# The low parts of a down projection's weights: a VectorE subtraction, or a negated copy and an adding transfer

## The chip, the cores and the metric

The kernel runs on one core of a Trainium2 chip. The time is the device time of one execution, in microseconds (us). The kernel before has a median of 911.25 us over 3 runs (911.24 to 911.4). All durations of single instructions come from one profiled execution, which took 911.68 us.

The engines are named as in the profile: PE is TensorE's matmul and PEld its weight load, DVE is VectorE, ACT is ScalarE, POOL is GpSimd, and SP is SyncE, which only issues transfers here. A trailing q (SPq, POOLq) means the engine's sequencer.

## The reference

A decoder block for 512 tokens of width 1024: attention with a sliding window, beside a gated linear recurrence; both are merged, projected and added to the input; a SwiGLU feed-forward with 2816 hidden columns follows, then a last normalisation. What matters here is its end:

```
z = (jax.nn.silu(jnp.einsum('bsd,df->bsf', u, w_ffn_gate[layer]))
     * jnp.einsum('bsd,df->bsf', u, w_ffn_up[layer]))
h = h + jnp.einsum('bsf,fd->bsd', z, w_ffn_down[layer])
...
return rmsnorm(h, norm_final_g)
```

All inputs are float32, `w_ffn_down` has 2816 x 1024 elements (11 MiB).

## The kernel before

Every product is made in three matmuls of a shorter format (fp32r). Each operand x is split into a high part h, which is x rounded to fp32r, and a low part l = x - h; then h·h + h·l + l·h stands for the product.

The weights go through the class `Weights`. They are read from DRAM in units of 1 MiB (`load`, lines 55 to 68) by SP's queue into a tile `raw` with two buffers. A unit has two granules of 128x1024. `split` (lines 79 to 104) makes the high and the low tile of one granule: ScalarE copies `raw` to `wh` with rounding (line 98), and VectorE subtracts, `wl` = `raw` - `wh` (line 102). `wh` and `wl` have three buffers each. `get` (lines 106 to 112) hands out the granules in order and splits up to `AHEAD` = 2 granules ahead of the one handed out. `split` also asks for the unit of its own granule and for the next one (lines 81 to 83).

The units are listed at lines 149 to 166. The last eleven are of kind "f": two blocks of 128 rows of `w_ffn_down`, each row whole, 1024 columns. Their 22 granules are the row blocks f = 0 to 21 of the down projection. The units before them are of kind "c" (gate and up weights).

The feed-forward loop (lines 834 to 851) handles two blocks of hidden columns at a time: two gate granules (VectorE line 839, a sigmoid on ScalarE, two multiplications on GpSimd at lines 843 and 844), then two up granules (VectorE line 849, ScalarE line 850, VectorE line 851). The first two granules of the down projection are split beside its last two up granules.

The down projection has two parts. For f = 0 to 17 (lines 874 to 877) each granule feeds 24 matmuls: four blocks of 128 tokens, three terms, two halves of 512 columns (`down`, line 866; the matmul is line 870). [...] The last `TAIL_F` = 4 granules are split into four buffers of their own, from the pool `wd` (lines 878 to 880); with them the four token blocks are finished one after the other (lines 881 to 913): the residual (line 891), sums of squares on ScalarE (line 892), the multiplication with the last gain on GpSimd (line 904), the power on GpSimd (line 908), the scaling on three engines and the store.

The order of an engine's instructions follows a scheduler that keeps the data's dependencies and works by its own estimate of times; the order of the program sets the priorities.

Of the kernel before, what the change touches and what calls it, by code (L numbers as in the profile page):

```python
# [15 lines left out]
F32 = mybir.dt.float32  # L16
F32R = mybir.dt.float32r
U32 = mybir.dt.uint32
AF = mybir.ActivationFunctionType
ALU = mybir.AluOpType  # L20
AX = mybir.AxisListType

P = 128
# [17 lines left out]
class Weights:  # L41


    def __init__(self, nc, pool, units):
# [7 lines left out]
        self.done = 0  # L52
        self.pos = 0

    def load(self, u):
        if u >= len(self.units) or u in self.raw:
            return
        kind, w, c0 = self.units[u]
        t = self.pool.tile([P, 2048], F32, tag="raw", bufs=2, name=f"raw{u}")
        if kind == "f":  # L60
            self.nc.sync.dma_start(
                t.rearrange("p (f n) -> p f n", f=2),
                w[c0 * P:(c0 + 2) * P, :].rearrange("(f p) n -> p f n", p=P))
        else:
            self.nc.sync.dma_start(
                t.rearrange("p (k n) -> p k n", k=KD),
                w[:, c0:c0 + 256].rearrange("(k p) n -> p k n", p=P))
        self.raw[u] = t
# [10 lines left out]
    def split(self, i, pool=None, bufs=3, high=None, low=None, low_after=None):  # L79
        u, kind, half = self.grans[i]  # L80
        self.load(u)
        if u:
            self.load(u + 1)
        nc, raw = self.nc, self.raw[u]
        if kind == "c":
            src = raw.rearrange("p (k n) -> p k n", k=KD)[:, :, half * P:(half + 1) * P]
            shape = dict(k=KD)
        else:
            n = 256 if kind == "k" else 1024
            src = raw[:, half * 1024:(half + 1) * 1024].rearrange("p (k n) -> p k n", n=n)  # L90
            shape = dict(n=n)
        pool = pool or self.pool
        h = pool.tile([P, 1024], F32R, tag="wh", bufs=bufs, name=f"wh{i}")
        l = pool.tile([P, 1024], F32R, tag="wl", bufs=bufs, name=f"wl{i}")
        hv = h.rearrange("p (k n) -> p k n", **shape)
        lv = l.rearrange("p (k n) -> p k n", **shape)
        if high is None:
            nc.scalar.activation(hv, src, AF.Copy)  # L98
        else:
            high.tensor_copy(hv, src)  # L100
        with low_after or nullcontext():
            (low or nc.vector).tensor_tensor(lv, src, hv.bitcast(F32), ALU.subtract)  # L102
        self.ready[i] = (hv, lv)
        self.done = i + 1

    def get(self, limit=None):
        i = self.pos
        self.pos += 1
        last = min(i + AHEAD, len(self.grans) - 1 if limit is None else limit)
        while self.done <= last:  # L110
            self.split(self.done)
        return self.ready.pop(i)
# [836 lines left out]
```

## Time and profile before

| what | value |
|---|---|
| median of 3 runs | 911.25 us |
| the profiled execution | 911.68 us |
| its span, first to last instruction | 910.0 us |
| mean granted TensorE clock | 0.999 |
| read from HBM, written to HBM | 82.90 MB, 2.10 MB |
| TensorE in the stage of the down projection | first matmul at 783.3 us, last at 902.6 us |
| transfers issued by GpSimd | none |

The profile is read like this. A row of the timeline has the start, the duration, the engine, the line of the kernel, the operation, the tile written and the tiles read (`wl<-raw,wh`), the shapes, and in brackets how long the engine was idle before and which event ended that. A row of the groups has the number of instructions, then their busy time in us and the mean of one in ns, then the idle time before them by what ended it. A row of the transfers has their count, the size of one, and the median time from issue to landing. A row of the windows has each engine's busy time in that stretch, the granted clock, the mean busy share of the sixteen transfer engines, and GB/s. The chain goes back from the last instruction, at each step to what released it. Matmul rows overlap (each shows 389 ns, one starts every 227 ns), so the stage's time is read from starts.

### The profile page before, as it was taken

The numbers are of one execution on the slowest core, as the hardware profiler recorded it, in microseconds if no ns is written. First come the engines' busy times: TensorE is split into PE (matmuls) and PEld (weight loads), VectorE is DVE, ScalarE is ACT, GpSimd is POOL, SyncE is SP. The second block draws the span as 40 slices with busy tenths as digits, with TensorE's granted clock in tenths as the row PEclk, the third lists the DMA queues.
The fourth block names the chain that finished last, engine by engine and source line by source line (L and its number), as shares of the span: only waits on it lengthen the run. The fifth ranks groups of instructions, "written<-read, shape, count | busy, mean of one in ns | idle before, by whom it ended". The sixth has DMA issues, their size and how long they took to land.

```text
span 910.0 us, 11601 instructions
## 1 busy us (share of the span) xinstructions
PE 899.6 (99%) x4668; PEld 769.8 (85%) x4668; DVE 463.3 (51%) x725; ACT 371.0 (41%) x634; POOL 142.8 (16%) x148
## 2 busy tenths in 40 slices
PE   8999999999999999999999999999999999999996
PEld 7888889888898988888888998888888888888885
DVE  5677877647484755745345445334443334322314
ACT  6566775655453636215233443223322223211214
POOL 3003533300000000000000003222233322100004
PEclk9999999999999999999999999999999999999999
DMA  7321211322221141322243222232222333322212
GB/s 257 93 93 47 94 47 47 93 93 93 93 91 49 47 139 47 95 91 94 93 167 110 94 93 93 93 93 93 92 93 94 101 109 111 119 93 93 92 47 94
DMA packets 73522, 85.74 MB, mean 94 GB/s; under 512 B 1690, under 2 KB 68348, under 8 KB 73468
## 3 DMA queue, kind: packets, MB, share of 16 engines
q1 hardware_dynamic: 72876, 83.95, 28.6%
q10 hardware_dynamic: 592, 1.05, 0.3%
q8 instruction: 37, 0.61, 0.3%
q14 instruction: 17, 0.14, 0.0%
HBM read 82.90 MB, written 2.10 MB: 93 GB/s over the span
## 4 chain that ended last, share of the span: by engine, by line
PE 97%; SPq 1%; DMA 0%; POOL 0%; DVE 0%; issue 0%; ACT 0%; POOLq 0%; DVEq 0%
PE acc L870 13%; PE ps_big L362 13%; PE ps_big L363 13%; PE ps_big L364 13%; PE ps_f L364 9%; PE ps_f L363 9%; PE ps_f L362 9%; PE ps_o L374 2%; PE ps_v L373 2%; PE ps_o L373 2%; PE ps_o L372 2%; PE ps_v L374 2%; PE ps_v L372 2%; PE pv L498 1%; PE sc L442 1%; PE pa L619 1%
## 5 line engine op out<-in xcount | busy, mean ns | idle before, releaser
L98 ACT ACTIVATE wh<-raw 128x1024 fp32r<-128x1024 f32 x147 | 155.1, 1059 | 394.8 <-PE ps_f L363 161.8
L102 DVE TENSOR_TENSOR wl<-raw,wh 128x1024 fp32r<-128x1024 f32 x147 | 180.4, 1229 | 160.1 <-ACT wh L98 159.9
L362 PE MATMUL ps_big<-uh,wh 128*128 128x512 f32 x376 | 148.8, 396 | 0.0
L363 PE MATMUL ps_big<-ul,wh 128*128 128x512 f32 x376 | 147.8, 393 | 0.0
L364 PE MATMUL ps_big<-uh,wl 128*128 128x512 f32 x376 | 147.7, 393 | 0.0
L363 PE MATMUL ps_f<-u2l,wh 128*128 128x512 f32 x352 | 137.2, 390 | 0.0
L364 PE MATMUL ps_f<-u2h,wl 128*128 128x512 f32 x352 | 136.9, 389 | 0.0
L362 PE MATMUL ps_f<-u2h,wh 128*128 128x512 f32 x352 | 136.8, 390 | 0.0
L364 PEld LDWEIGHTS ps_big<-uh,wl 128*128 128x128 f32 x376 | 70.7, 188 | 14.2
L363 PEld LDWEIGHTS ps_big<-ul,wh 128*128 128x128 f32 x376 | 70.8, 188 | 13.6
L362 PEld LDWEIGHTS ps_big<-uh,wh 128*128 128x128 f32 x376 | 70.7, 188 | 13.5
L363 PEld LDWEIGHTS ps_f<-u2l,wh 128*128 128x128 f32 x352 | 66.1, 188 | 14.0 <-issue 0.2
L364 PEld LDWEIGHTS ps_f<-u2h,wl 128*128 128x128 f32 x352 | 66.1, 188 | 13.8 <-issue 0.2
L362 PEld LDWEIGHTS ps_f<-u2h,wh 128*128 128x128 f32 x352 | 66.1, 188 | 13.7
L843 POOL TENSOR_TENSOR zg<-zg,sgf 128x512 f32<-128x512 f32 x22 | 39.4, 1794 | 161.0 <-ACT sgf L134 161.0
L870 PE MATMUL acc<-wh,zl 128*128 128x512 f32 x176 | 56.9, 389 | 0.0
L870 PE MATMUL acc<-wl,zh 128*128 128x512 f32 x176 | 56.9, 389 | 0.0
L870 PE MATMUL acc<-wh,zh 128*128 128x512 f32 x176 | 56.8, 389 | 0.0
L849 DVE TENSOR_TENSOR zz<-ps_f,zg 128x512 f32<-128x512 f32 x22 | 15.2, 692 | 62.6 <-PE ps_f L364 61.5
L839 DVE TENSOR_TENSOR zg<-ps_f,R 128x512 f32<-128x512 f32 x22 | 15.1, 691 | 62.2 <-PE ps_f L364 62.2
L248 POOL TENSOR_TENSOR r<-ss,neghalf 128x4 f32<-128x4 f32 x8 | 10.1, 1260 | 232.8 <-DVE ss L247 232.8
L870 PEld LDWEIGHTS acc<-wh,zh 128*128 128x128 f32 x176 | 33.0, 188 | 6.9
(222 smaller groups left out, 1560.0 us busy)
## 6 DMA issues: line engine op xcount, KB each, us to landing
raw<-in_w_in_dram SPq DMA_DIRECT2D x27, 1024.0 KB, 5.2
raw<-in_w_ffn_gate_dram SPq DMA_DIRECT2D x11, 1024.0 KB, 5.0
raw<-in_w_ffn_up_dram SPq DMA_DIRECT2D x11, 1024.0 KB, 5.1
raw<-in_w_ffn_down_dram SPq DMA_DIRECT2D x11, 1024.0 KB, 4.8
raw<-in_w_branch_attn_dram SPq DMA_DIRECT2D x4, 1024.0 KB, 6.0
raw<-in_w_branch_hgrn_dram SPq DMA_DIRECT2D x4, 1024.0 KB, 4.9
raw<-in_w_out_dram SPq DMA_DIRECT2D x4, 1024.0 KB, 5.2
xt<-in_x_dram SPq DMA_DIRECT2D x4, 512.0 KB, 7.7
```

Source lines behind the costliest of these rows:

```text
L98: nc.scalar.activation(hv, src, AF.Copy)
L102: (low or nc.vector).tensor_tensor(lv, src, hv.bitcast(F32), ALU.subtract)
L362: pe.matmul(ps, wh[:, k, :], ah[:, k, :], start=k == 0, stop=False)
L363: pe.matmul(ps, wh[:, k, :], al[:, k, :], start=False, stop=False)
L364: pe.matmul(ps, wl[:, k, :], ah[:, k, :], start=False, stop=k == KD - 1)
L372: pe.matmul(ps, ah[:, k0 + k, ts], wh[:, k, :], start=first and k == 0, stop=False)
L373: pe.matmul(ps, ah[:, k0 + k, ts], wl[:, k, :], start=False, stop=False)
L374: pe.matmul(ps, al[:, k0 + k, ts], wh[:, k, :], start=False, stop=last and k == 3)
L839: tt(zg, fproject((lambda: row_broadcast(R, rstd2, u2pool)) if first else None), R, ALU.mult)
L843: pool_e.tensor_tensor(zg, zg, sg, ALU.mult)
L849: tt(z, fproject(), gs[a], ALU.mult)
L870: pe.matmul(acc[t][half], ah[:, f, ts], wv[:, 0, half * S:half * S + S], start=f == 0 and ah is zh and wv is wh, stop=f == NF - 1 and ah i ...
```

## The change

For the granules of kind "f", the 22 of the down projection, the low tile is made in another way. ScalarE writes -h to it (a copy of `wh` with scale -1), and a transfer issued by GpSimd adds the same weights, read once more from DRAM, onto the tile: l = -h + w. The high copy at line 98 and the load into `raw` stay. All other weights are split as before. Each of the 22 transfers moves 512 KB (128 rows of 4 KB).

```
--- before.py
+++ after.py
@@ -51,6 +51,8 @@
         self.ready = {}
         self.done = 0
         self.pos = 0
+
+        self.by_dma = next(u for u, k in enumerate(units) if k[0] == "f")
 
     def load(self, u):
         if u >= len(self.units) or u in self.raw:
@@ -98,10 +100,26 @@
             nc.scalar.activation(hv, src, AF.Copy)
         else:
             high.tensor_copy(hv, src)
-        with low_after or nullcontext():
-            (low or nc.vector).tensor_tensor(lv, src, hv.bitcast(F32), ALU.subtract)
+        if u >= self.by_dma:
+            self.hv = hv
+            self.low_by_dma(i, lv, src)
+        else:
+            with low_after or nullcontext():
+                (low or nc.vector).tensor_tensor(lv, src, hv.bitcast(F32), ALU.subtract)
         self.ready[i] = (hv, lv)
         self.done = i + 1
+
+    def low_by_dma(self, i, lv, src):
+
+        u, kind, half = self.grans[i]
+        _, w, c0 = self.units[u]
+        nc, hv = self.nc, self.hv
+        nc.scalar.activation(lv, hv.bitcast(F32), AF.Copy, scale=-1.0)
+        if kind == "c":
+            d = w[:, c0 + half * P:c0 + half * P + P].rearrange("(k p) n -> p k n", p=P)
+        else:
+            d = w[(c0 + half) * P:(c0 + half + 1) * P, :].rearrange("(f p) n -> p f n", p=P)
+        nc.gpsimd.dma_start(lv, d, accum_op=ALU.add)
 
     def get(self, limit=None):
         i = self.pos
```

## The prediction

> **What bounds the kernel now.** I read the page's head and its chain first, to see which engine sets the end.
>
> ```profile
> span 910.0 us, 11601 instructions
> ...
> PE 899.6 (99%) x4668; PEld 769.8 (85%) x4668; DVE 463.3 (51%) x725; ACT 371.0 (41%) x634; POOL 142.8 (16%) x148
> ...
> PE 97%; SPq 1%; DMA 0%; POOL 0%; DVE 0%; issue 0%; ACT 0%; POOLq 0%; DVEq 0%
> ```
>
> TensorE is busy for 99% of the span, and 97% of the chain that ended last is TensorE itself. So shorter work on another engine is worth something only where TensorE waits for it. The change touches the last stage alone; the view of windows and the chain in order of time show that stage.
>
> ```profile
> core 0: us, PE busy (x) PEld busy (x) DVE busy (x) ACT busy (x) POOL busy (x), PEclk, DMA share, GB/s
> 783.30:881.30 98.00, 98.00 (x435) 81.12 (x433) 25.70 (x24) 21.41 (x21) 0.00 (x0) 1.00 0.29 96
> 881.30:903.00 21.70, 21.69 (x96) 17.64 (x94) 8.79 (x25) 8.38 (x31) 8.59 (x10) 1.00 0.19 74
> ```
>
> ```profile
> 783.32 119.69 PE acc L870 x528
> 903.03 0.44 DVE yo L891
> ...
> 905.70 0.39 DVEq L945
> ```
>
> The reader is to see that TensorE has no gap between 783.30 and 903.00 (98.00 of 98.00 us, then 21.69 of 21.70), at granted clock 1.00. The down projection is one piece of the chain: 528 matmuls in 119.69 us, or 0.2267 us each. One row block f of its weights (a granule: one high and one low tile of 128x1024) feeds 24 of them, so a granule lasts 5.44 us. There is no wait that the change could remove, and its VectorE work is not in the chain. The 7 us behind the last matmul hold no granule's work.
>
> **What the change removes.** The groups of the window 789 to 876 us, where only this stage runs:
>
> ```profile
> L102 DVE TENSOR_TENSOR wl<-raw,wh 128x1024 fp32r<-128x1024 f32 x19 | 23.1, 1225 | 64.2 <-ACT wh L98 64.2
> L98 ACT ACTIVATE wh<-raw 128x1024 fp32r<-128x1024 f32 x19 | 19.9, 1059 | 67.4 <-PE acc L870 62.5 <-DMA raw<-in_w_ffn_down_dram 4.9
> ```
>
> Removed are 22 subtractions of 1.225 us, 27 us of VectorE. VectorE is busy for 25.70 of 98.00 us there and TensorE never waits for it, so they bring 0. Added are 22 ScalarE activations of the same shape as the high copies, at 1.059 us each: 23.3 us on an engine busy for 21.41 of 98.00 us. Both ops of a granule take 2.1 us of its 5.44, so ScalarE does not become the bound.
>
> **Steady state: the slack of a granule.** The timeline of ScalarE:
>
> ```profile
> 772.29 1.06 ACT L98 ACTIVATE wh<-raw 128x1024 fp32r<-128x1024 f32 x1 [3.85 <-PE ps_f L363]
> 773.26 0.63 ACT L134 ACTIVATE sgf<-zg 128x512 f32<-128x512 f32 x1
> 777.75 1.06 ACT L98 ACTIVATE wh<-raw 128x1024 fp32r<-128x1024 f32 x1 [3.85 <-PE ps_f L363]
> 778.71 0.63 ACT L129 ACTIVATE zh<-zz 128x512 fp32r<-128x512 f32 x1
> 783.17 1.06 ACT L98 ACTIVATE wh<-raw 128x1024 fp32r<-128x1024 f32 x1 [3.83 <-PE ps_f L363]
> ...
> 848.63 1.06 ACT L98 ACTIVATE wh<-raw 128x1024 fp32r<-128x1024 f32 x1 [4.38 <-PE acc L870]
> 854.07 1.06 ACT L98 ACTIVATE wh<-raw 128x1024 fp32r<-128x1024 f32 x1 [4.38 <-PE acc L870]
> 859.51 1.06 ACT L98 ACTIVATE wh<-raw 128x1024 fp32r<-128x1024 f32 x1 [4.38 <-PE acc L870]
> 861.41 2.01 ACT L98 ACTIVATE wh<-raw 128x1024 fp32r<-128x1024 f32 x2 [0.84 <-DMA raw<-in_w_ffn_down_dram]
> 864.95 1.06 ACT L98 ACTIVATE wh<-raw 128x1024 fp32r<-128x1024 f32 x1 [1.53 <-PE acc L870]
> 870.07 2.01 ACT L98 ACTIVATE wh<-raw 128x1024 fp32r<-128x1024 f32 x2 [4.06 <-DMA raw<-in_w_ffn_down_dram]
> ```
>
> The first three rows at L98 are f=0, 1 and 2; from 848.63 they are f=14, 15 and 16, then a pair of the last four (18, 19), f=17, and the other pair (20, 21). The copies of f=14 to 16 start when TensorE has let go of a buffer (every 5.44 us), and three buffers mean that the new tiles are wanted two granules later: 10.88 us after the release, plus 0.45 for the low part, since two matmuls on the high part come first. Today the two ops fill 0.1 + 1.06 + 1.23 us of it. Afterwards 0.1 + 2.1 us go to ScalarE, and the GpSimd issue and the transfer have 11.33 - 2.2 = 9.1 us. That wait, TensorE for a landing, is the new one.
>
> **What the adding transfer costs.** No transfer issued by GpSimd and no adding one is in this trace. The nearest rows are of the transfers by size, and of SP's queue in the window 783 to 880 us:
>
> ```profile
> raw<-in_w_ffn_down_dram SPq DMA_DIRECT2D x11, 1024.0 KB, 4.8
> ...
> xt<-in_x_dram SPq DMA_DIRECT2D x4, 512.0 KB, 7.7
> ...
> out_dram<-yo ACTq DMA_DIRECT2D x4, 256.0 KB, 2.5
> ```
>
> ```profile
> q1 hardware_dynamic: 2479, 9.50, 29.0%
> ```
>
> The queue row says 29.0% of 97 us for 9.50 MB: 3.1 us of all sixteen engines for a 1 MiB load, which lands 4.8 us after its issue, so 1.7 us are start and end. A plain 512 KB load would occupy 1.55 us: the lower end. The adding transfer must read 512 KB from DRAM and 512 KB from the tile, as many bytes as the 1 MiB load reads. I take 3.1 us of the engines and 4.8 us to landing, which is nearest to that row. The upper end is the slowest 512 KB transfer of the trace, 7.7 us to landing for x (four in a row with others beside them), 6.0 without start and end. [...]
>
> For the GpSimd issue I take its one-column instruction at L908, 0.55 us; the bounds are nothing and 2.4 us, its slowest row, at the kernel's start:
>
> ```profile
> 773.97 1.79 POOL L843 TENSOR_TENSOR zg<-zg,sgf 128x512 f32<-128x512 f32 x1 [2.27 <-ACT sgf L134]
> 775.84 1.29 POOL L844 TENSOR_TENSOR zg<-zg,R 128x512 f32<-128x512 f32 x1
> 888.27 1.99 POOL L904 TENSOR_TENSOR yo<-yo,gfin 128x512 f32<-128x512 f32 x2 [111.14 <-ACT jkd L129]
> 890.22 0.55 POOL L908 TENSOR_TENSOR r1d<-s1d,neghalf 128x1 f32<-128x1 f32 x1
> ```
>
> ```profile
> 10.09 2.40 POOL L102 TENSOR_TENSOR wl<-raw,wh 128x1024 fp32r<-128x1024 f32 x1 [1.97 <-ACT wh L98]
> ```
>
> So a transfer alone is there after 0.55 + 4.8 = 5.4 us of 9.1. GpSimd has nothing else from 777.1 to 888.3 us, so nothing is queued behind the waiting issues but the next issue.
>
> Two transfers share the engines with the 1 MiB load of each unit (two granules, 10.88 us): 3.1 + 2 x 3.1 = 9.3 us of 10.88. The load starts behind the odd granule's high copy and its adding transfer a microsecond later, so that one can be held up by the load's 3.1 us: 5.4 + 3.1 = 8.5 of 9.1. It fits, by 0.6 us. **The point from which the stage slows is 3.1 + 2a = 10.88, a = 3.9 us of engine time for one adding transfer.**
>
> **Raw buffers and SP.** The queue's own waits:
>
> ```profile
> SPq L61 <- DVE wl L102: 107.4, 11, 10.6
> ```
>
> SP's loads wait for the subtraction, the last reader of a raw tile. Now the high copy is the last reader, so a load starts 1.2 us earlier. That gains nothing for TensorE; it only moves the load's start closer to the transfer of the granule before.
>
> **The ends of the stage.** At the front, f=0: ScalarE has both ops done by about 774.9 (the sigmoid between them), but GpSimd may do its two multiplications first, to 777.1. With 5.4 us the tile lands at 782.5; it is wanted at 783.32 + 0.45 = 783.8. It holds, by 1.3 us. f=1 has 2 us more.
>
> At the back, the last four granules have buffers of their own and are split as soon as their weights are there. From 862 us five things are to be moved: the transfers of f=16, 18, 19 and 17 and the last load, 5 x 3.1 = 15.5 us, so to 877.7, and 0.8 for the end, 878.5, if f=17 comes last. Its low part is wanted at 783.32 + 17 x 5.44 + 0.45 = 876.3. That is a stall of up to 2.2 us; with 2.5 us for an adding transfer it is 0, as it is where f=17 is issued ahead of 19. I take 0.8 us. f=21, the last, is there by 884.5 by the same count of 3.1 us each, wanted at 883.5 plus that shift, and adds next to nothing.
>
> **The sum.** 911.68 us in the profiled execution (span 910.0, 1.7 around it) lies 0.4 above the median of the runs, 911.25. Removed VectorE work 0, ScalarE 0, steady transfers 0, front 0, back +0.8: 911.25 + 0.8 = **912.0 us**, within what the measurement of this kernel can tell from no change (0.2%, 1.8 us).
>
> **The rivals.**
>
> *Rate: the engines become the bound, slower.* If an adding transfer occupies a > 3.9 us, a unit takes 3.1 + 2a, and nine units run through the steady part. At a = 4.5, 12.1 us a unit, +1.2 x 9 = +11, 922 us. At the upper end of 6.0, 15.1, +4.2 x 9 = +38, 949 us. For it speaks that no row shows an adding transfer or descriptors written by GpSimd; against it, that the load's 3.1 us for the same bytes leave 20% of room. [...]
>
> *A single late landing, slower.* The first transfer may be longer than the others (something loaded or set up at first use), or the back may crowd as worked out above. A first transfer of 10 us instead of 5.4 is late by 3.3 us; with the back's 2.2 that is up to +5.5; 914 to 917 us, typically 915.
>
> *Faster.* It would need a wait of TensorE that VectorE ends; there is none in the 120 us. Only a rearrangement outside the stage could do it: 909 us.
>
> *That it does not do what it says:* the subtractions go, but since TensorE never waits for them, this and the forecast cannot be told apart by time; both give 911 to 912.
>
> **How the numbers follow.** Forecast (all hidden, or a stall below 1.8 us), 0.50, with its own range of 910.3 to 913. Single late landing, 0.19. Rate, 0.27, half of it above 935 us. Faster, 0.04. So faster 0.04, same 0.50, slower 0.46. The range goes from 909.8 to 940: left out are most of the faster case and the part of the rate case above 940, about 0.15 together.
>
> **What would show it.** Right: the down projection is still one piece of 528 matmuls of about 119.7 us, the rows at L102 lose 22 subtractions, ScalarE gains 22 activations of 1.06 us, and landings of GpSimd's 512 KB transfers are near 5 us alone and 8 beside a load. Rate wrong: TensorE waits for the landing of wl in every unit, at even distances, with the DMA share near 1 in the stage. Late landing: one gap at 783 us or one at 876 us, and none between. The prediction falls if the engines' time for an adding transfer is above 3.9 us, or if GpSimd's issue takes several microseconds.

## The result

| | kernel before | changed kernel |
|---|---|---|
| median | 911.25 us (4 runs) | 915.97 us (4 runs, 915.47 to 916.95) |
| ratio, 95% interval | | 1.0053 [1.0041, 1.0065] |
| the profiled execution | 911.68 us | 915.47 us |
| its span | 910.0 us | 913.7 us |

The change costs 4.7 us, 0.5%, and the interval lies clear of 1. The forecast was 912.0; the range, 909.8 to 940, holds the time, while the forecast's own range, 910.3 to 913, does not. Ratios here and below leave out a single execution, of the kernel "Both cuts" below, which took 1392.39 us at a mean granted clock of 0.61.

### The profile page after: what moved, and what is told of

Same layout as the page of the kernel before. It is cut to its first block, busy times and chain, and to the rows that moved or that the text cites. A ratio compares the mean times of both kernels' runs of the same rounds, so it can differ in the third digit from the quotient of the medians.

```text
span 913.7 us, 11638 instructions
## 1 busy us (share of the span) xinstructions
PE 901.7 (99%) x4668; PEld 771.2 (84%) x4668; DVE 436.6 (48%) x703; ACT 393.4 (43%) x656; POOL 161.6 (18%) x170
## 4 chain that ended last, share of the span: by engine, by line
PE 95%; DMA 1%; SPq 1%; issue 1%; POOL 0%; ACT 0%; DVE 0%; POOLq 0%; DVEq 0%
PE ps_big L380 13%; PE ps_big L382 13%; PE ps_big L381 13%; PE acc L888 11%; PE ps_f L381 9%; PE ps_f L380 9%; PE ps_f L382 9%; PE ps_o L392 2%; PE ps_o L391 2%; PE ps_v L391 2%; PE ps_o L390 2%; PE ps_v L392 2%; PE ps_v L390 2%; PE pv L516 1%; DMA wl<-in_w_ffn_down_dram 1%
## 5 line engine op out<-in xcount | busy, mean ns | idle before, releaser
L108 DVE TENSOR_TENSOR wl<-raw,wh 128x1024 fp32r<-128x1024 f32 x125 | 153.7, 1230 | 95.3 <-ACT wh L100 95.1
L380 PEld LDWEIGHTS ps_big<-uh,wh 128*128 128x128 f32 x376 | 70.7, 188 | 13.5
L909 DVE TENSOR_TENSOR yo<-acc,hn 128x256 f32<-128x256 f32 x16 | 5.9, 417 | 108.6 <-PE acc L888 108.6
```

Source lines behind the costliest of these rows:

```text
L380: pe.matmul(ps, wh[:, k, :], ah[:, k, :], start=k == 0, stop=False)
```

## The profile after

The page's head, and the queue that is new:

```profile
span 913.7 us, 11638 instructions
...
PE 901.7 (99%) x4668; PEld 771.2 (84%) x4668; DVE 436.6 (48%) x703; ACT 393.4 (43%) x656; POOL 161.6 (18%) x170
...
q0 software_dynamic: 3168, 11.54, 7.1%
...
wl<-in_w_ffn_down_dram POOLq DMA_DIRECT2D x22, 512.0 KB, 6.5
```

VectorE lost 26.7 us of busy time, ScalarE gained 22.4. One adding transfer occupies the sixteen engines for 7.1% x 913.7 / 22 = 2.95 us, and lands 6.5 us after its issue in the median. The windows of the last stage (columns as before):

```profile
783.30:881.30 98.00, 95.94 (x416) 78.68 (x415) 1.00 (x4) 41.14 (x41) 17.42 (x20) 0.98 0.89 201
881.30:903.00 21.70, 21.70 (x97) 18.00 (x96) 7.39 (x21) 6.70 (x26) 7.11 (x9) 1.00 0.18 58
```

TensorE now has 2.06 us of idle time, the mean granted clock of the stretch is 0.98, and the transfer engines are busy for 0.89 of it (0.29 before). The chain in order of time puts the gap in one place:

```profile
782.74 70.96 PE acc L888 x312
853.72 1.07 ACT wh L100
854.81 1.07 ACT wl L117
855.88 0.28 issue
856.17 0.87 POOL wl L122
857.04 6.64 issue
863.73 0.84 POOL wl L122
864.64 9.19 DMA wl<-in_w_ffn_down_dram
873.88 32.73 PE acc L888 x136
```

From 782.74 to 906.61 the stage takes 123.9 us; it was 119.7. (The stage starts 0.6 us earlier in this execution, so the span grew by less.) TensorE waits for one landing, at 873.88. What stands out ahead of it is the row of 6.64 us: from 857.04 to 863.7 GpSimd had nothing to issue; between two granules of the steady part it is idle for 4.57 us. The timelines of ScalarE and GpSimd show why (a row with x3 is three instructions in a row):

```profile
853.72 1.06 ACT L100 ACTIVATE wh<-raw 128x1024 fp32r<-128x1024 f32 x1 [3.29 <-PE acc L888]
854.81 1.06 ACT L117 ACTIVATE wl<-wh 128x1024 fp32r<-128x1024 f32 x1
859.50 2.96 ACT L100 ACTIVATE wh<-raw 128x1024 fp32r<-128x1024 f32 x3 [3.62 <-DMA raw<-in_w_ffn_down_dram]
862.36 2.94 ACT L117 ACTIVATE wl<-wh 128x1024 fp32r<-128x1024 f32 x3
```

```profile
856.17 0.87 POOL L122 DMA_DIRECT2D wl<-in_w_ffn_down_dram  x1 [4.57 <-ACT wl L117]
863.70 2.77 POOL L122 DMA_DIRECT2D wl<-in_w_ffn_down_dram  x3 [6.66 <-ACT wl L117]
```

Up to f = 15 a copy is followed by its own negation. Then the program has on ScalarE: copy of f = 18, copy of 16, copy of 19, and only then the negations of 18, 16 and 19. The trace shows three copies in a row and then three negations; the first copy waits for a load (to 859.50), while f = 16's weights had come with an earlier one; and the landing that ends TensorE's wait for f = 16 is that of the second of three transfers. So f = 16's negation stands behind three copies. Its transfer is issued at 864.6 us; in the rhythm of the steady part it would be 861.6. It shares the transfer engines with that of f = 18 and with the last 1 MiB load, lands at 873.8, and f = 16 is wanted from 869.8 on. The scheduler had placed f = 16's eight matmuls on the high part first; that covers 1.8 us.

Behind the gap TensorE runs slower. Windows of one microsecond:

```profile
872.00:873.00 1.00, 0.00 (x0) 0.00 (x0) 0.00 (x0) 0.00 (x0) 0.87 (x1) 1.00 1.05 205
873.00:874.00 1.00, 0.12 (x1) 0.12 (x2) 0.00 (x0) 0.00 (x0) 0.00 (x0) 1.00 0.99 197
874.00:875.00 1.00, 1.00 (x4) 0.82 (x5) 0.00 (x0) 0.00 (x0) 0.00 (x0) 0.75 1.04 205
875.00:876.00 1.00, 1.00 (x4) 0.81 (x3) 0.00 (x0) 0.00 (x0) 0.00 (x0) 0.50 1.11 221
876.00:877.00 1.00, 1.00 (x4) 0.71 (x4) 0.00 (x0) 0.00 (x0) 0.00 (x0) 0.50 1.15 229
877.00:878.00 1.00, 1.00 (x4) 0.81 (x3) 0.00 (x0) 0.00 (x0) 0.00 (x0) 0.54 1.01 197
878.00:879.00 1.00, 1.00 (x6) 0.81 (x5) 0.00 (x0) 0.00 (x0) 0.00 (x0) 1.00 0.99 197
```

The column behind POOL is the granted clock: half speed from 874.5 to 877.9. The missing clock adds up to 0.25 + 0.50 + 0.50 + 0.46 = 1.7 us. So of the 4.2 us 2.06 are the gap and 1.7 the clock; 0.4 is left, as it is in the experiment below with a gap of 2.0 us and no loss of clock (2.4 us in all). TensorE's weight load (PEld) waits 2.48 us for the same landing, 0.4 more than the matmul.

## The experiments

Theory A: ScalarE's order delays f = 16. Theory B: the last six transfers and the last load crowd the transfer engines. Theory C: a gap of TensorE costs its length and some time at a lower clock; theory D: the lower clock came with the transfers' traffic. Theory E: the loss comes from bunches of transfers and too little time ahead; theory F: from the traffic itself. Each kernel was timed beside the kernel before, at 911.3 to 911.4 us.

**The last four granules by VectorE.**

```
-        if u >= self.by_dma:
+        if u >= self.by_dma and i < len(self.grans) - TAIL_F:
```

> The change without its last four granules: the low parts of f = 18 to 21 are subtracted by VectorE as before, f = 0 to 17 by the adding transfer. On ScalarE f = 18's copy still stands ahead of f = 16's, as in the changed kernel. Theory A (the order on ScalarE delays f = 16, its transfer is issued some 2 us late, and that alone makes the wait): a gap of 1 us or more on TensorE near 872 us stays, 913 to 915 us. Theory B (the transfers of f = 18 and 19 take the engines from that of f = 16): they are gone, f = 16 is issued near 863.6 us and lands by 870.5 us, beside the last 1 MiB load alone; no gap, 911.0 to 911.7 us. Steady part, both: no wait.

Measured: 914.37 us, 1.0030 [1.0018, 1.0042]. TensorE's waits, in us in total, times, the longest:

```profile
PE acc L888 <- DMA wl<-in_w_ffn_down_dram: 1.4, 2, 1.2
```

The gap of 1.2 us is at f = 16 again: its transfer is issued at 866.58 in this run, behind the three copies, and lands 8.3 us later. The time lies in theory A's range, and a gap needs no transfers of f = 18 and 19. But they add to it: f = 16's transfer is issued 8.46 us behind f = 15's here and 8.47 in the changed kernel, and lands after 8.3 us instead of 9.2, with a gap of 1.2 us instead of 2.06. The stage takes 121.9 us in this execution, 2.2 more than before; another 0.9 us lies ahead of the stage, so the time alone would say too much. The other wait, 0.2 us, is in the steady part at 811.9 us, behind a landing of 9.0 us.

**The order on ScalarE alone.** The last four granules' work is kept behind the negation of f = 16; all 22 adding transfers stay.

```
-        W.split(i, wd, TAIL_F)
+        with tc.issue_after(W.negs[first - 2]):
+            W.split(i, wd, TAIL_F)
```

> The whole change, with the last four granules kept behind f = 16's negation on ScalarE, so that f = 16's copy and negation come first. All 22 adding transfers stay. Theory A: f = 16's transfer is issued near 861.6 us, as in the steady part, and lands near 868; no gap at f = 16; 911.0 to 911.8 us. Theory B: the six last transfers and the last load still crowd, 12 us of engine time from 864.7 us on, so f = 17 (wanted between 876.3 and 877.7) lands near 877.4: a gap of 0 to 1.1 us there, and with the clock that follows a gap 912 to 914 us.

Measured: 914.32 us, 1.0044 [1.0031, 1.0058]. In the chain f = 16 is no longer there, but f = 17 is:

```profile
866.13 1.07 ACT wl L118
867.20 0.28 issue
867.48 11.15 DMA wl<-in_w_ffn_down_dram
878.67 26.18 PE acc L890 x114
```

A landing of 11.15 us, and a gap of 1.8 us, with the clock at 1.00 behind it. That is the crowd of theory B, at the granule that it named, larger than the 0 to 1.1 us that it gave. (This is one of the shorter executions, 913.7 us; the six go from 913.55 to 917.5.) So each theory is right for one granule, and mending one lets the other appear. In the changed kernel itself the gap at f = 16 comes first, and everything behind it is wanted later; that this is why no second gap of that size shows there is an argument, not a measurement.

**Both cuts.** The order as in the second experiment, and the last four by VectorE as in the first.

> Both cuts at once: the last four granules' low parts by VectorE, and their ScalarE work kept behind f = 16's negation; f = 0 to 17 by the adding transfer. If the loss of the changed kernel is the two causes at the back (f = 16 late by ScalarE's order, f = 17 late by the crowd of transfers) and nothing else: no gap at the back, 911.2 to 911.8 us. If the steady part loses too (its margin is 9.1 us against landings of up to 9 us after the issue), some runs stay 0.5 to 2 us above that, with gaps of a few tenths anywhere between 795 and 870 us.

Measured: 911.95 us, 1.0008 [0.9998, 1.0017], not to be told from the kernel before by this interval. No gap is left at the back. One of 0.2 us is in the steady part (waits of TensorE in this kernel):

```profile
PE acc L890 <- DMA wl<-in_w_ffn_down_dram: 0.2, 1, 0.2
```

That is the expectation's second case: of its ten executions four took 912.5 to 913.8 us; of the 21 of the kernel before, one did (913.09).

**Only the last four by the adding transfer.**

```
-        if u >= self.by_dma:
+        if i >= len(self.grans) - TAIL_F:
```

> Only the last four granules by the adding transfer, f = 0 to 17 by VectorE as before. Their tiles are wanted at 881 to 884 us and their transfers issued by 873. Two causes at the back: neither f = 16 nor f = 17 needs a transfer, so no gap: 911.0 to 911.7 us. If the last four transfers were late themselves, a gap near 881 us of 1 to 3 us and 913 to 916 us.

Measured: 911.56 us, 1.0001 [0.9992, 1.0010], and the 528 matmuls in one piece of 119.69 us. With nothing else adding, the last four transfers are in time; in the changed kernel they harm those in front of them.

**More time ahead.** From f = 2 on, the four buffers of `wd`, three granules ahead.

```
+        if last - TAIL_F < i < last:
+            W.split(i)
+        else:
+            W.split(i, wd, 4)
...
+        while W.done <= min(W.pos + 3, last):
+            split_next()
```

> All 22 adding transfers, with more room in time: from f = 2 on the tiles come from the pool of four that only the last granules had, and are split three granules ahead (the last four take turns with the old three buffers). A transfer then has some 14.5 us instead of 9.1 from the negation to the first use. If the loss is late landings, all gaps go: 911.0 to 911.8 us. If it is the engines' rate (traffic above what sixteen engines carry), the time stays at 914 us or more.

Measured: 915.28 us, 1.0038 [1.0025, 1.0050], outside the first expectation and in the second's range, but for another reason. The chain shows no gap at the back, but a new one at the front:

```profile
783.01 1.12 ACT wh L100 x2
...
788.68 9.33 DMA wl<-in_w_ffn_down_dram
798.01 0.04 issue
798.05 107.30 PE acc L888 x472
```

With four buffers free at once, four copies stood in front of four negations on ScalarE (783.0 to 791.2), four transfers were issued from 788.68 on, and f = 2 came 2.4 us late. Behind that gap the clock stayed at 1.00, and 472 matmuls ran without another gap at a DMA share near 0.9. So not the rate, but a bunch, in another place.

**More time ahead, and the order.** The same, with each copy kept behind the negation of the granule before.

```
+            with self.tc.issue_after(self.neg) if self.neg else nullcontext():
+                nc.scalar.activation(hv, src, AF.Copy)
```

> All 22 adding transfers with four buffers and three granules ahead, and on ScalarE each granule's copy kept behind the negation of the granule before, so that no copies stand in front of an older negation. Theory E (the loss is bursts: adding transfers released in a bunch by ScalarE's order, against too little time ahead): f = 2 is issued near 785.5 us instead of 788.7 and lands before 794.5; no gap anywhere, one piece of 528 matmuls, 911.0 to 911.7 us, as fast as the kernel before and not faster. Theory F (the adding transfers' traffic itself, 85 to 90% of the engines' time, costs TensorE something): 913 us or more.

Measured: 911.77 us, 1.0004 [0.9995, 1.0013]. The stage's piece of the chain and its window:

```profile
782.62 119.89 PE acc L892 x528
```

```profile
783.00:881.00 98.00, 98.00 (x433) 80.94 (x432) 1.18 (x4) 41.71 (x41) 17.47 (x20) 1.00 0.90 203
```

All 22 adding transfers, transfer engines busy for 0.90, and no gap. That is the change at its best: as fast as the kernel before, not faster. Theory F, which needed 913 us or more, falls; the time is 0.07 us above the range that theory E gave. Single landings still take up to 13.5 us here (7.4 in the median), but with three granules ahead they are in time.

**The order with the old buffers.** The same rule for ScalarE in the changed kernel.

> The changed kernel with the same order on ScalarE but its old buffers: f = 16 and 17 come first, the last four behind them. No gap at f = 16 or 17. The last four transfers are then issued between 869 and 878 us with the last load beside them: by engine time they are done near 886 us, and f = 21 is wanted at 883.5. Theory E: a gap of 1 to 3 us near 882 to 885 us, 912.5 to 915 us. If time ahead does not matter once the order is right: 911.0 to 911.8 us.

Measured: 914.59 us, 1.0034 [1.0023, 1.0046]. The chain ends its wait at 885.96 us, behind the last transfer (issued at 877.89, landed after 8.02 us; the gap is 1.3 us, with one of 0.5 us before it):

```profile
877.89 8.02 DMA wl<-in_w_ffn_down_dram
885.96 19.58 PE acc L892 x85
```

As theory E has it: with the order alone the bunch moves to the last granules.

**A gap without transfers.** In the kernel before, the subtraction of f = 16 is repeated, seven or eight times in all.

```
+            for _ in range(7 if i == len(self.grans) - TAIL_F - 2 else 1):
+                (low or nc.vector).tensor_tensor(lv, src, hv.bitcast(F32), ALU.subtract)
```

> The kernel before, without any adding transfer; f = 16's subtraction is done seven times over on VectorE, so that its low part is ready near 873.4 us, about 1.2 us after TensorE has done what it can without it. Theory C (any gap of TensorE of this length costs its own length and some microseconds at a lower granted clock behind it): loss of 1.2 us of gap and about 2 us of clock, 913.9 to 914.9 us, with a granted clock of 0.5 to 0.7 in the 4 us behind the gap. Theory D (the lower clock in the changed kernel came with the transfers' traffic): only the gap, 912.2 to 912.8 us, clock 1.00.

> As the one before, with eight subtractions: f = 16's low part is ready near 875.7 us, a gap of about 3.4 us. Theory C: 3.4 us and about 2 us of clock, 916.2 to 917.2 us (the clock's part does not grow with the gap). Theory D: 914.4 to 915.0 us, clock 1.00.

Measured: 913.98 us, 1.0028 [1.0017, 1.0039], and 917.68 us, 1.0071 [1.0058, 1.0084]. TensorE's gaps are 2.0 and 4.4 us. Windows of two microseconds, first of the kernel with seven subtractions, then of the one with eight:

```profile
872.00:874.00 2.00, 0.37 (x2) 0.33 (x3) 2.00 (x3) 0.13 (x1) 0.00 (x0) 1.00 0.00 0
874.00:876.00 2.00, 2.00 (x10) 1.65 (x9) 0.71 (x1) 0.00 (x0) 0.00 (x0) 1.00 0.00 0
```

```profile
874.00:876.00 2.00, 0.02 (x1) 0.02 (x1) 1.93 (x2) 0.00 (x0) 0.00 (x0) 0.52 0.00 0
876.00:878.00 2.00, 2.00 (x5) 1.61 (x6) 0.00 (x0) 0.00 (x0) 0.00 (x0) 0.50 0.00 0
878.00:880.00 2.00, 2.00 (x7) 1.52 (x6) 0.00 (x0) 0.00 (x0) 0.00 (x0) 0.50 0.00 0
880.00:882.00 2.00, 2.00 (x8) 1.63 (x7) 0.00 (x0) 0.00 (x0) 0.00 (x0) 0.77 0.00 0
```

With the gap of 4.4 us the clock is halved with no transfer running (last two columns 0.00 and 0): theory D falls, here the lower clock came with the gap alone. After 2.0 us it stays at 1.00 here, while the changed kernel had it halved after 2.06. So theory C holds for the long gap; near 2 us both outcomes occur, and what tells them apart was not shown. The time of the first lies in C's range by a longer gap than expected (2.0 us for 1.2), not by its clock; the second lies 0.5 us above C's range, with a gap of 4.4 us for 3.4, and with 2.5 us of missing clock behind it; C had taken that part as not growing with the gap, and it was 1.7 in the changed kernel.

**A plain copy in place of the adding one.** The low tiles then hold w instead of w - h.

```
-        nc.gpsimd.dma_start(lv, d, accum_op=ALU.add)
+        nc.gpsimd.dma_start(lv, d)
```

> The same 22 transfers from GpSimd as plain copies without the addition: the low tiles then hold the weights themselves instead of w - h, the rest of the work is the same. If an addition costs because the tile is read as well, the engines' time of one transfer falls from 2.95 us to about 1.5 us, the landing from 6.5 to about 4.5 us, and the gap at f = 16 shrinks below 0.5 us (911.2 to 912 us). If the transfer is slow because GpSimd writes its descriptors, both stay.

Measured: 911.48 us in one run, no gap. Queue and landing:

```profile
q0 software_dynamic: 3168, 11.54, 3.9%
...
wl<-in_w_ffn_down_dram POOLq DMA_DIRECT2D x22, 512.0 KB, 5.1
```

3.9% x 909.8 / 22 = 1.61 us of the engines, against 2.95 with the addition: 1.83 times. The price comes with the addition, not with GpSimd as the issuer; what in the addition costs was not shown. The order on ScalarE is that of the changed kernel (GpSimd's longest wait for a negation is 7.2 us, 6.7 there), but no copy lands later than 6.8 us after its issue, and TensorE does not wait. So the order alone makes no gap; it needs the dear transfer too.

**The adding transfer twice.** The low tiles then hold 2w - h.

> The changed kernel with each adding transfer done twice, one after the other (the low tiles then hold 2w - h). A granule then needs 2 x 2.95 us of the engines, a unit 3.1 + 4 x 2.95 = 14.9 us against 10.88 us of TensorE's work. By the prediction's point for the rate (more than 10.88 us a unit): gaps in every unit, 4 us each over nine units, 36 us, and with the lower clock behind gaps of 2 us and more up to 15 us besides: 945 to 970 us, DMA share above 0.95 in the stage. If only bursts counted: under 925 us.

Measured: 975.56 us in one run, above the expectation's 970. TensorE's waits:

```profile
PE acc L889 <- DMA wl<-in_w_ffn_down_dram: 43.8, 12, 6.2
```

12 waits, 43.8 us, and a mean clock of 0.91 from 783 to 900 us and 0.86 from 900 to 960. The DMA share is 0.90 and 0.74 there, not above 0.95 as expected: each second transfer waits for the first to land (20 waits of GpSimd, 76.4 us in all), so this is rate and latency together. It shows that the stage breaks with twice the transfers, and not where the rate alone becomes the bound.

## Why the prediction was right or wrong

- *What bounds the kernel, and what the change removes*: right. 26.7 us less VectorE work and 22.4 us more on ScalarE moved nothing; with the landings in time all 22 transfers give 911.77 us.
- *The price of an adding transfer*: right. 3.1 us of the engines and 5.4 us to landing were taken; 2.95 and, where undisturbed, 5.3 were measured. The issue on GpSimd takes 0.87 us instead of 0.55 (0.54 for the plain copy).
- *Rate*: right that it is not the bound, though the point of 3.9 us a transfer was not tried. 3.1 + 2 x 2.95 = 9.0 us a unit, 0.83 of 10.88; the window shows 0.89 with no gap before f = 16.
- *Steady slack of 9.1 us, left 0.6*: right for the changed kernel (7.7 us at most from f = 2 to 15), and as thin as that: two other profiles have a landing of 9.0 us there and a gap of 0.2.
- *The front*: right, f = 0 landed at 780.4 us and was in time.
- **The back: this step failed.** The prediction saw the crowd and named f = 17, with a stall of up to 2.2 us (2.0 by its own figures, since 862 + 15.5 is 877.5), and took 0.8. The second experiment has that stall at 1.8 us. But it took ScalarE's order from the trace of before, f = 16 first; the new program has the copies of f = 18, 16 and 19 ahead of their negations, so f = 16 is late first, by 2.06 us after 1.8 us of cover, some 1.2 of it without the transfers of f = 18 and 19 and 0.9 with them. And it priced a gap at its own length: the halved clock and the 0.4 us that are left made 4.2 us of 2.06.
- *The rivals*: what happened is the single late landing (914 to 917 us, typically 915), given 0.19, and not the forecast, given 0.50. Slower had 0.46. That the range holds the time is in part luck: it reaches to 940 for the rate rival, which did not come, and the sum behind 912.0 missed the granule that was late.

## What to carry to other kernels

When work moves into a transfer whose result TensorE waits for, count the time from the last step that releases it, and look for places where the releasing steps of several tiles are bunched: at 0.90 of the transfer engines' time all 22 transfers were in time with the order on ScalarE and three granules ahead together; with one of the two or neither a bunch was late, by gaps of 1.3 to 2.4 us. An engine's order in the old trace is no safe sign of the order in the new program; ask what the scheduler can put in front. A gap of TensorE of about two microseconds cost twice its length in one of these kernels and little more than its length in another: 4.2 us for 2.06, and 2.4 for 2.0.

## What the runs showed of the hardware

A gap of 2.06 us (changed kernel) was followed by half the granted clock for 3.4 us, from 874.5 to 877.9 us. With one of 4.4 us (eight subtractions) the clock was at half for 6.8 us, from 874.1 to 880.9, the first 1.9 us of it within the gap. Behind gaps of 1.8 us (the order on ScalarE alone), 2.0 us (seven subtractions) and 2.4 us (more time ahead) it stayed at 1.00. The kernel with doubled transfers has two gaps of nearly one length, each ended by a landing:

```profile
822.05 0.72 PE L889 MATMUL acc<-wl,zh 128*128 128x512 f32 x2 [2.76 <-DMA wl<-in_w_ffn_down_dram]
...
830.59 1.22 PE L889 MATMUL acc<-wl,zh 128*128 128x512 f32 x2 [2.78 <-DMA wl<-in_w_ffn_down_dram]
```

```profile
820.00:825.00 5.00, 2.95 (x13) 2.44 (x14) 0.00 (x0) 0.00 (x0) 1.04 (x2) 1.00 1.05 200
825.00:830.00 5.00, 2.80 (x13) 1.99 (x11) 0.00 (x0) 2.12 (x2) 2.31 (x3) 1.00 1.03 189
830.00:835.00 5.00, 4.42 (x12) 3.53 (x13) 0.00 (x0) 0.00 (x0) 0.13 (x1) 0.66 0.95 242
```

Behind the first, of 2.76 us, the clock is 1.00 up to 830 us; behind the second, of 2.78 us, its mean is 0.66 from 830 to 835 us. So in these traces the length of a gap does not settle what it costs in clock, and what does was not shown.

The addition made a 512 KB transfer from GpSimd 1.83 times as dear (2.95 us of the engines for 1.61). The plain copies from GpSimd cost the engines nearly what SP's loads did for the same bytes: 1.61 us for 512 KB against 3.1 us for 1 MiB.
